# Up-projection of both MLPs by one level of Strassen's scheme, in four rounds

## The chip, the core and the metric

The kernel runs on one core of a Trainium2 chip. Its time is the device time of one execution in microseconds (us), taken on the chip; lower is better. TensorE (PE, with its weight loads as PEld) multiplies, VectorE (DVE) and ScalarE (ACT) work elementwise, GpSimd (POOL) does little here, and SyncE (SP) issues the transfers.

## The reference

Two layers over 16 meta tokens and 512 real ones, model width 1024, hidden width 4096, all in float32. Each layer is a mixer (stick-breaking attention in layer 0, a gated linear recurrence in layer 1) and then an MLP; a last norm closes it. What is changed is the MLP:

```python
def sq_relu_mlp(x, w_up, w_down):
    hdn = jax.nn.relu(x @ w_up)
    return (hdn * hdn) @ w_down
for i in range(DEPTH):
    ...
    hn = rms_norm(h, norm_mlp[i])
    h = h + sq_relu_mlp(hn, mlp_w_up[i], mlp_w_down[i])
h = rms_norm(h, norm_final)
return h[:, N_META:]
```

## The kernel before, in words

Activations lie transposed: the 1024 channels are 8 chunks of 128 partitions, the tokens are columns. Layer 0 works on all 528 columns, as two blocks of 264 (`ALL`, since one PSUM bank holds 512 floats); the second MLP and the output need the 512 real columns alone (`REAL`), one block of 512.

A float32 product is made of three fp32r products. `split` (L56 to L61) makes a rounded high part on ACT (L58) and the remainder on DVE (L61); `gemm` (L100) issues high by high, high by low and low by high for each 128x128 weight tile, all of them at L98. `load_unit` (L88) loads 512 KB of weights, 128 by 1024, into one of three `raw` buffers and splits it into `whi` and `wlo` (two buffers each).

At the end of the attention layer the output projection writes the residual stream: `hs<-z` or `hs<-g` at L545, per chunk of 128 channels and block of 264 columns. Per chunk `xs_write` scales by the gain and splits (ACT L128, DVE L129), and `Norm.add` squares on ACT and accumulates on DVE (L152). These eight pairs of `x` tiles are the input of the first MLP. The norm's factor `rstd` (L154 to L160: a product with ones, a square root on ACT, a reciprocal on DVE) is multiplied in after the first product.

`mlp` (L583) has two halves of 16 hidden chunks. In the up phase of a half each of 16 units gives one hidden chunk: 48 matmuls of 264 columns in layer 0 or 24 of 512 in layer 1, then `t` = max(g, 0)·rstd on DVE (L605), two squares on ACT (L608, L609) and `hl` on DVE (L610). In the down phase each of the 8 output chunks takes 16 hidden chunks, two units, and is added to `hs` (L637). In the very last chunk of layer 1 the two column halves are worked one after the other, and `last` (L804) makes the final norm, the multiplications (L829, L831) and the output transfers (L834) of each half.

Instructions are written in program order, and a scheduler interleaves them by priorities; what it arrived at is fixed when the kernel is built. Each engine then takes its queue strictly in that order. Weight loads and splits are raised in priority (`HP`).

Of the kernel before, what the change touches and what calls it, by code (L numbers as in the profile page):

```python
# [40 lines left out]
def tile_hybrid_trunk(ctx: ExitStack, tc: tile.TileContext, h0, vec, wqk, wv, wo, wob,  # L42
# [120 lines left out]
    xs_mlp0 = []  # L163
    hs = [None, None]

    def h_chunk(c):
        return hs[c // 4][:, c % 4, :]

    def attention_layer():
# [394 lines left out]
        x4 = [vqp.tile([P, 4, T], F32R, tag=t, name="x4") for t in ("v2", "v2", "q", "q")]  # L564
        xs_mlp0.append([x4[c // 4][:, c % 4, :] for c in range(KC)])
        xs_mlp0.append([x4[2 + c // 4][:, c % 4, :] for c in range(KC)])
        xs["h"], xs["l"] = xs_mlp0

        def final(m):
            xs_write(m, h_chunk(m), V_MLP0)  # L570
            nrm.add(m, h_chunk(m))
# [10 lines left out]
    def mlp(l, cols, nrm, done, xh, xl, gtile, last=None):

        c0a = cols[0][0]
        nb = len(cols)
        cw = cols[0][1]
        with ExitStack() as c2:
            hp = c2.enter_context(tc.tile_pool(name="hid", bufs=1))
            r3 = None
            hh = [hp.tile([P, T], F32R, name=f"hh{f}") for f in range(16)]  # L590
            hl = [hp.tile([P, T], F32R, name=f"hl{f}") for f in range(16)]
            for half in range(2):
                for f in range(16):
                    hi, lo = load_unit(wup[l, 16 * half + f])
# [1 line left out]
                    gemm([g[:, i, 0:w] for i, (_, w) in enumerate(cols)], cols,
                         [(hi[:, k * P:(k + 1) * P], lo[:, k * P:(k + 1) * P], xh[k], xl[k]) for k in range(KC)])
                    if r3 is None:
                        gs = gtile()
                        rstd = nrm.finish([gs[:, i, 0:w] for i, (_, w) in enumerate(cols)], cols)  # L600
                        r3 = rstd[:, c0a:T].rearrange("p (b w) -> p b w", b=nb)
                    t = hp.tile([P, T], F32, tag="t", name="t", bufs=2)
                    t3 = t[:, c0a:T].rearrange("p (b w) -> p b w", b=nb)
                    for i in range(nb):
                        dve.scalar_tensor_tensor(out=t3[:, i, :], in0=g[:, i, 0:cw], scalar=0.0, in1=r3[:, i, :],  # L605
                                                 op0=ALU.max, op1=ALU.mult)
                    r = hp.tile([P, T], F32, tag="r", name="r", bufs=2)
                    act.activation(out=hh[f][:, c0a:T], in_=t[:, c0a:T], func=AF.Square)  # L608
                    act.activation(out=r[:, c0a:T], in_=t[:, c0a:T], func=AF.Square)  # L609
                    dve.tensor_tensor(out=hl[f][:, c0a:T], in0=r[:, c0a:T], in1=f32(hh[f][:, c0a:T]),  # L610
                                      op=ALU.subtract)
                for m in range(KC):
                    us = [load_unit(wdn[l, half, m, j]) for j in range(2)]
                    g = gtile()
                    ks = [(us[k // 8][0][:, (k % 8) * P:(k % 8 + 1) * P], us[k // 8][1][:, (k % 8) * P:(k % 8 + 1) * P],
                           hh[k], hl[k]) for k in range(16)]
                    if last and half == 1 and m == KC - 1:
                        gs = [g[:, 0, 0:S // 2], gtile()[:, 0, 0:S // 2]]
                        cs = [NM, NM + S // 2]
                        gemm([gs[0]], [(cs[0], S // 2)], ks)  # L620
                        fin = [last(i, gtile()) for i in range(2)]
                        n = (0, 3, 8, 16)
                        for i in range(2):
                            next(fin[i])
                        for i in range(2):
                            hc = h_chunk(m)[:, cs[i]:cs[i] + S // 2]
                            b = ()
                            with tc.high_priority(HP * i):
                                dve.tensor_tensor(out=hc, in0=gs[i], in1=hc, op=ALU.add)
                                for j in range(3):  # L630
                                    if i == 0:
                                        gemm([gs[1]], [(cs[1], S // 2)], ks[n[j]:n[j + 1]], j == 0, j == 2, b)
                                    b = next(fin[i], ())
                        continue
                    gemm([g[:, i, 0:w] for i, (_, w) in enumerate(cols)], cols, ks)
                    h3 = h_chunk(m)[:, c0a:T].rearrange("p (b w) -> p b w", b=nb)
                    dve.tensor_tensor(out=h3, in0=g[:, 0:nb, 0:cw], in1=h3, op=ALU.add)  # L637
                    if half == 1:
                        done(m, h_chunk(m))
# [257 lines left out]
```

## Time and profile before

| | us |
|---|---|
| median of three runs | 1231.8 (1231.26 to 1233.49) |
| the profiled execution | 1233.84 |
| its span, first to last instruction | 1231.9 |
| PE busy in the span | 1205.1 |
| DVE busy | 672.6 |
| ACT busy | 558.4 |

The granted clock of TensorE has a mean of 0.993 over the span. The first MLP runs from 329.64 us to about 704.8, the second from 862.9 to 1221.7; the attention layer lies before, the recurrent mixer and its output projection between them. Busy times are of the records' own durations; since matmuls and DVE instructions overlap with their successors, the distance from one start to the next is what a queue of them takes.

### The profile page before, as it was taken

The page shows a single profiled execution, that of the slowest core. Times are in us where ns is not written, and L with a number is a line of the kernel's source. Part 1 is how long each engine was busy: PE and PEld are TensorE (multiplying, and loading weights), DVE is VectorE, ACT ScalarE, POOL GpSimd, SP SyncE. Part 2 cuts the span into 40 slices and gives each one's busy share as a digit, 9 for nine tenths or more (in the row PEclk, how much of TensorE's full clock was granted, in tenths as well). Part 3 has the DMA queues.
Part 4 walks back from the last instruction along what each step waited for, and adds up shares of the span by engine and source line. Part 5 has one row for each costly group of instructions (what it writes and reads, how often), then busy time and mean ns, then how long its engine had stood idle before and what let it go on. Part 6 is the DMA issues. An engine that isn't in the chain of part 4 may idle for free.

```text
span 1231.9 us, 19086 instructions
## 1 busy us (share of the span) xinstructions
PE 1205.1 (98%) x7932; PEld 1110.6 (90%) x7932; DVE 672.6 (55%) x1121; ACT 558.4 (45%) x927; POOL 15.5 (1%) x33
## 2 busy tenths in 40 slices
PE   7999999999999999999999999999999999999997
PEld 7999999998999999999999998878888888888886
DVE  7887878796754432344433487585544223444333
ACT  6777777786533311133323348663434121433321
POOL 3000000000000000000000000000000000000000
PEclk9999999999999999999999999999999999999998
DMA  6221213042223222322323231223232233232322
GB/s 219 85 82 57 82 35 89 17 122 69 87 89 101 87 86 87 103 86 87 99 74 103 86 120 63 75 69 119 87 101 88 86 103 103 86 103 86 103 86 69
DMA packets 33334, 110.14 MB, mean 89 GB/s; under 512 B 3936, under 2 KB 5984, under 8 KB 33248
## 3 DMA queue, kind: packets, MB, share of 16 engines
q1 hardware_dynamic: 32816, 108.53, 27.7%
q8 instruction: 62, 1.02, 0.3%
q10 hardware_dynamic: 432, 0.39, 0.1%
q14 instruction: 24, 0.20, 0.1%
HBM read 102.49 MB, written 2.10 MB: 85 GB/s over the span
## 4 chain that ended last, share of the span: by engine, by line
PE 90%; DVE 5%; ACT 3%; issue 2%; DMA 1%; SPq 0%; DVEq 0%; ACTq 0%
PE g L98 79%; PE z L98 9%; PE o L98 2%; DVE wlo L61 1%; ACT whi L58 1%; DVE th L715 1%; ACT r L79 0%; DVE i L714 0%; DMA hs<-in_h_dram 0%; DVE xl L129 0%; ACT th L79 0%; DVE y L749 0%; DMA q<-q 0%; ACT L79 0%; DVE rstd L159 0%
## 5 line engine op out<-in xcount | busy, mean ns | idle before, releaser
L58 ACT ACTIVATE whi<-raw 128x1024 fp32r<-128x1024 f32 (+1 forms) x178 | 186.7, 1050 | 550.3 <-PE g L98 288.0
L61 DVE TENSOR_TENSOR wlo<-raw,whi 128x1024 fp32r<-128x1024 f32 (+1 forms) x178 | 215.6, 1212 | 257.2 <-PE g L98 131.8
L98 PE MATMUL g<-xh,whi 128*128 128x264 f32 (+1 forms) x720 | 230.5, 335 | 0.5 <-DVE v L354 0.4
L98 PE MATMUL g<-xl,whi 128*128 128x264 f32 (+1 forms) x720 | 230.4, 334 | 0.0
L98 PE MATMUL g<-hh,whi 128*128 128x264 f32 (+2 forms) x784 | 229.3, 318 | 0.0
L98 PE MATMUL g<-hl,whi 128*128 128x264 f32 (+2 forms) x784 | 229.2, 318 | 0.0
L98 PEld LDWEIGHTS g<-hl,whi 128*128 128x128 f32 x784 | 147.5, 188 | 11.2
L98 PE MATMUL g<-xh,wlo 128*128 128x264 f32 (+1 forms) x720 | 156.8, 335 | 0.8 <-DVE wlo L61 0.8
L98 PEld LDWEIGHTS g<-hh,whi 128*128 128x128 f32 x784 | 147.6, 188 | 10.8
L98 PEld LDWEIGHTS g<-xh,whi 128*128 128x128 f32 x720 | 135.9, 189 | 15.2 <-PE z L98 0.5
L98 PEld LDWEIGHTS g<-xl,whi 128*128 128x128 f32 x720 | 135.9, 189 | 14.0 <-issue 0.2
L605 DVE SCALAR_TENSOR_TENSOR t<-g,rstd 128x264 f32<-128x264 f32 (+1 forms) x96 | 46.7, 515 | 172.4 <-PE g L98 172.3
L98 PE MATMUL g<-x,whi 128*128 128x264 f32 x1024 | 137.5, 284 | 0.8 <-DVE hs L545 0.8
L98 PE MATMUL g<-hh,wlo 128*128 128x264 f32 (+2 forms) x784 | 136.7, 319 | 0.0
L98 PEld LDWEIGHTS g<-x,whi 128*128 128x128 f32 x1024 | 130.7, 188 | 1.1 <-ACT sq L151 1.0
L98 PEld LDWEIGHTS g<-xh,wlo 128*128 128x128 f32 x720 | 117.5, 188 | 15.0 <-DVE wlo L61 1.1
L98 PEld LDWEIGHTS g<-hh,wlo 128*128 128x128 f32 x784 | 115.5, 188 | 10.8
L98 PE MATMUL g<-x,wlo 128*128 128x264 f32 x512 | 78.4, 285 | 0.0
L98 PEld LDWEIGHTS g<-x,wlo 128*128 128x128 f32 x512 | 69.2, 188 | 0.1
L79 ACT ACTIVATE sp<-sp 128x288 f32<-128x288 f32 (+3 forms) x128 | 62.2, 510 | 1.3
L98 PE MATMUL g<-vhi,xl 128*128 128x256 f32 x160 | 46.1, 289 | 0.0
L98 PE MATMUL g<-vhi,xh 128*128 128x256 f32 x160 | 46.1, 288 | 0.0
(189 smaller groups left out, 1607.4 us busy)
## 6 DMA issues: line engine op xcount, KB each, us to landing
raw<-in_wup_dram SPq DMA_DIRECT2D x64, 512.0 KB, 3.3
raw<-in_wdn_dram SPq DMA_DIRECT2D x64, 512.0 KB, 3.3
raw<-in_win_dram SPq DMA_DIRECT2D x16, 512.0 KB, 3.4
raw<-in_wqk_dram SPq DMA_DIRECT2D x14, 512.0 KB, 3.5
q<-q SPq DMA_DIRECT2D x16, 264.0 KB, 4.5
raw<-in_wv_dram SPq DMA_DIRECT2D x8, 512.0 KB, 3.4
raw<-in_wo_dram SPq DMA_DIRECT2D x8, 512.0 KB, 3.4
raw<-in_wout_dram SPq DMA_DIRECT2D x8, 512.0 KB, 3.3
```

The source lines that it names most:

```text
L58: act.activation(out=hi, in_=src, func=AF.Copy)
L61: (lo_eng or dve).tensor_tensor(out=lo, in0=src, in1=f32(hi), op=ALU.subtract)
L79: ins = act.activation(out=out, in_=in_, func=func, **kw)
L98: return pe.matmul(out=o, lhsT=lhsT, rhs=rhs, start=start, stop=stop, skip_group_check=True)
L605: dve.scalar_tensor_tensor(out=t3[:, i, :], in0=g[:, i, 0:cw], scalar=0.0, in1=r3[:, i, :], op0=ALU.max, op1=ALU.mult)
L715: dve.tensor_tensor_scan(out=ths[n], data0=rs[n], data1=is_[n], initial=0.0, op0=ALU.mult, op1=ALU.add)
```

## The change

The up-projection `x @ w_up` is cut into 2 by 2 blocks: the 1024 input channels into an upper and a lower half of 4 chunks, two hidden chunks at a time (a pair), the token columns into two blocks of 264 (layer 0) or 256 (layer 1, `HALVES`). Instead of eight block products a pair takes seven, in the form with 15 additions that is due to Winograd. Each block product is 4 chunks by 3 fp32r products, 12 matmuls; a pair has 84.

- `Blocks` makes the inputs' operands: `B11`, `B21` (scaled columns), `N22` (a negated block) and the differences `T1` to `T4`, each split into high and low. It takes the place of `xs_write` at the end of the attention layer and of the mixer. Chunk k and chunk k+4 go together; `upper` does the first, `lower` the second.
- `up_weights` makes a pair's weight operands: of two loaded units the sums `S1`, `P2`, `P3`, `P4`, split like the others.
- `up_pair` issues the products into four accumulators a, b, d, c (two PSUM tiles), combines them through `u2` and `v` on DVE, applies `rstd`, and squares.
- The MLP has four rounds, each of 4 pairs (8 hidden chunks) and a down phase of 8 output chunks with 8 hidden chunks each. The down products keep their number; `hs` is added to 32 times a layer instead of 16.
- At the end of the last round output chunks 6 and 7 are worked by column halves: 6 and 7 of the first half, then 6 and 7 of the second.
- Buffers: `vqp` lives through the kernel and its tiles are shared by tags, the slots of `xh`/`xl` also hold `hh`/`hl` and mixer tiles, high and low parts of the attention's `s` and `w` share one tile. One attention mask is a slice of another, three POOL instructions less. The host lays `w_down` out by rounds.

The core of the diff; of the old `mlp` only the listing above is shown:

```diff
+    class Blocks:
...
+        def scaled(self, c, h_c, x):
+            (a, w), _ = self.cols
+            act.activation(out=x, in_=h_c[:, a:a + 2 * w].rearrange("p (b w) -> p b w", b=2), func=AF.Copy,
+                           scale=vecs[:, self.g0 + c:self.g0 + c + 1])
+        def upper(self, k, h_c):
+            w = self.cols[0][1]
+            x2 = pair(6, [P, 4, HT], F32, "x2")
+            self.x, self.y = x2[:, 0:2, 0:w], x2[:, 2:4, 0:w]
+            self.d = pair(7, [P, 4, HT], F32, "t4")[:, :, 0:w]
+            self.scaled(k, h_c, self.x)
+            dve.tensor_tensor(out=self.d[:, 0, :], in0=self.x[:, 1, :], in1=self.x[:, 0, :], op=ALU.subtract)
+            split(self.x[:, 0, :], *self.op["B11"][k])
+            split(self.d[:, 0, :], *self.op["T1"][k])
+        def lower(self, k, h_c):
+            x, y, d = self.x, self.y, self.d
+            self.scaled(4 + k, h_c, y)
+            dve.tensor_tensor(out=d[:, 1, :], in0=y[:, 1, :], in1=d[:, 0, :], op=ALU.subtract)
+            dve.tensor_tensor(out=d[:, 2, :], in0=x[:, 1, :], in1=y[:, 1, :], op=ALU.subtract)
+            dve.tensor_tensor(out=d[:, 3, :], in0=y[:, 0, :], in1=d[:, 1, :], op=ALU.subtract)
+            hi, lo = self.t[k]
+            split(d[:, 1:4, :], hi[:, 1:4, :], lo[:, 1:4, :])
+            split(y[:, 0, :], *self.op["B21"][k])
+            hi, lo = self.op["N22"][k]
+            act.activation(out=hi, in_=y[:, 1, :], func=AF.Copy, scale=-1.0)
+            dve.scalar_tensor_tensor(out=lo, in0=y[:, 1, :], scalar=-1.0, in1=f32(hi), op0=ALU.mult, op1=ALU.subtract)
...
+            if m in (0, 1, 2, 3):
+                blocks.upper(m, h_chunk(m))
+            if m in (0, 1, 2, 7):
+                blocks.lower(m % 4, h_chunk(m % 4 + 4))
+            nrm.add(m, h_chunk(m))
...
+            def up_weights(p):
+                with tc.high_priority(HP):
+                    a1, a2 = (wp.tile([P, 2 * H], F32, tag="raw", name="raw", bufs=3) for _ in range(2))
+                    for i, a in enumerate((a1, a2)):
+                        nc.sync.dma_start(out=a, in_=wup[l, 2 * p + i])
...
+                    split(a1, *hl_[0])
+                    dve.tensor_tensor(out=pq[:, H:], in0=a1[:, 0:H], in1=a2[:, 0:H], op=ALU.add)
+                    dve.tensor_tensor(out=a2[:, 0:H], in0=a2[:, 0:H], in1=a2[:, H:], op=ALU.add)
+                    split(a2, *hl_[1])
+                    dve.tensor_tensor(out=pq[:, 0:H], in0=a2[:, 0:H], in1=a1[:, 0:H], op=ALU.add)
+                    split(pq, *hl_[2])
+                    dve.tensor_tensor(out=p4, in0=pq[:, 0:H], in1=a1[:, H:], op=ALU.add)
+                    split(p4, *hl_[3])
...
+            def up_pair(p, hid):
+                W = up_weights(p)
+                g1, g2 = gtile(), gtile()
+                a, b, d, c = (g[:, i, 0:w] for g in (g1, g2) for i in range(2))
+                def prod(o, left, right, start):
+                    hi, lo = W[left]
+                    for k in range(4):
+                        x, xl_ = op[right][k]
+                        mm(o, hi[:, k * P:(k + 1) * P], x, start and k == 0, False)
+                        mm(o, hi[:, k * P:(k + 1) * P], xl_, False, False)
+                        mm(o, lo[:, k * P:(k + 1) * P], x, False, k == 3)
...
+                prod(a, "A11", "B11", True)
+                act.activation(out=n1, in_=a, func=AF.Copy)
+                yield
+                prod(d, "S1", "T1", True)
+                yield
+                prod(b, "P2", "T2", True)
+                dve.tensor_tensor(out=u2, in0=b, in1=n1, op=ALU.subtract)
+                prod(c, "P3", "T3", True)
+                v = t[:, 3, :]
+                dve.tensor_tensor(out=v, in0=c, in1=u2, op=ALU.add)
+                dve.tensor_tensor(out=v, in0=d, in1=v, op=ALU.add)
+                prod(a, "A12", "B21", False)
+                r3 = st["r3"]
+                dve.scalar_tensor_tensor(out=t[:, 0, :], in0=a, scalar=0.0, in1=r3[:, 0, :], op0=ALU.max, op1=ALU.mult)
+                prod(c, "A22", "T4", False)
+                prod(d, "P4", "N22", False)
+                for i, x in enumerate((d, c)):
+                    dve.tensor_tensor(out=t[:, 1 + i, :], in0=x, in1=u2, op=ALU.add)
+                dve.scalar_tensor_tensor(out=t[:, 1, :], in0=t[:, 1, :], scalar=0.0, in1=r3[:, 1, :],
+                                         op0=ALU.min, op1=ALU.mult)
+                dve.scalar_tensor_tensor(out=t[:, 2:4, :], in0=t[:, 2:4, :], scalar=0.0, in1=r3,
+                                         op0=ALU.max, op1=ALU.mult)
+                for i in range(2):
+                    h_, l_ = (x[:, c0a:T].rearrange("p (b w) -> p b w", b=2) for x in hid[i])
+                    x = t[:, 2 * i:2 * i + 2, :]
+                    act.activation(out=h_, in_=x, func=AF.Square)
+                    act.activation(out=x, in_=x, func=AF.Square)
+                    dve.tensor_tensor(out=l_, in0=x, in1=f32(h_), op=ALU.subtract)
+                yield
...
+            for q in range(4):
+                gens = [up_pair(4 * q + j, [(hh[2 * j + i], hl[2 * j + i]) for i in range(2)]) for j in range(4)]
+                if q == 0:
+                    next(gens[0])
+                    next(gens[0])
+                    next(gens[1])
+                    gs = gtile()
+                    rstd = nrm.finish([gs[:, i, 0:w] for i in range(2)], cols)
+                    st["r3"] = rstd[:, c0a:T].rearrange("p (b w) -> p b w", b=2)
+                for g in gens:
+                    for _ in g:
+                        pass
+                first = [(down_ks(q, m), gtile()) for m in range(2)]
+                for part in (slice(0, 6), slice(6, 8)):
+                    for m, (ks, g) in enumerate(first):
+                        gemm(down_outs(g), dcols, ks[part], part.start == 0, part.stop == 8)
+                        if part.stop == 8:
+                            down_end(q, m, g)
...
+    mlp(1, HALVES, REAL, nrm, blocks, done1, gtile, last)
```

Three places show how the order of the queues moves.

DVE where the attention layer ends and the first MLP begins, before: `hs` sums (L545), `x4` splits (L129), the norm's `acc` (L152), and a weight split (L61).

```order
L152 TENSOR_TENSOR acc_4071<-acc_4071,sq_4330 128x528
L545 TENSOR_TENSOR hs_3868<-g_4341,hs_3868 128x264
L129 SCALAR_TENSOR_TENSOR x4_4074<-hs_3868,vecs_70,x4_4072 128x528
L545 TENSOR_TENSOR hs_4078<-z_4388,xr_4354 128x264
L152 TENSOR_TENSOR acc_4071<-acc_4071,sq_4351 128x528
L61 TENSOR_TENSOR wlo_4535<-raw_4532,whi_4534 128x1024
L129 SCALAR_TENSOR_TENSOR x4_4075<-hs_4078,vecs_70,x4_4073 128x528
L152 TENSOR_TENSOR acc_4071<-acc_4071,sq_4416 128x528
```

The same place now, the last rows up to the split of `T2` to `T4` of the fourth chunk pair (`xt_3941`, 792 wide): `t4` are the differences, `pq`, `p4` and `o1l`, `o2l` the second pair's weight sums and splits.

```order
L66 TENSOR_TENSOR xb_3945<-x2_4263,xb_3945 128x264
L225 SCALAR_TENSOR_TENSOR xn_3947<-x2_4263,xn_3947 128x264
L210 TENSOR_TENSOR t4_4264<-x2_4263 128x264
L218 TENSOR_TENSOR t4_4264<-x2_4263 128x264
L665 TENSOR_TENSOR pq_4434<-raw_4431,raw_4430 128x512
L217 TENSOR_TENSOR t4_4264<-x2_4263,t4_4264 128x264
L66 TENSOR_TENSOR o1l_4439<-raw_4431,o1_4438 128x1024
L66 TENSOR_TENSOR xt_3941<-t4_4264,xt_3941 128x264
L667 TENSOR_TENSOR p4_4435<-pq_4434,raw_4430 128x512
L219 TENSOR_TENSOR t4_4264<-x2_4263,t4_4264 128x264
L66 TENSOR_TENSOR o2l_4441<-pq_4434,o2_4440 128x1024
L66 TENSOR_TENSOR xt_3941<-t4_4264,xt_3941 128x792
```

Weight operands and input operands now alternate in one queue. From the first `hs<-z` of the output projection to the last row shown there are 78 instructions: 8 of 1024 columns, 4 of 792, 7 of 528, 9 of 512, and 50 of 264, two of these reciprocals.

PE at the start of the first MLP, before: any chunk's products of one unit follow one another.

```order
L98 MATMUL g_4538<-x4_4072,whi_4534 128x264
L98 MATMUL g_4538<-x4_4074,whi_4534 128x264
L98 MATMUL g_4538<-x4_4073,whi_4534 128x264
L98 MATMUL g_4538<-x4_4075,whi_4534 128x264
L98 MATMUL g_4538<-x4_4073,whi_4534 128x264
```

Now: the first two pairs interleaved (`g_4400`, `g_4401` hold a, b, d, c of the first, `g_4456`, `g_4457` of the second).

```order
L103 MATMUL g_4401<-xt_3940,o2l_4385 128x264
L103 MATMUL g_4457<-xt_3941,o1_4438 128x264
L103 MATMUL g_4457<-xt_3941,o1l_4439 128x264
L103 MATMUL g_4457<-xt_3938,o2_4440 128x264 x2
L103 MATMUL g_4400<-xt_3941,o2_4384 128x264
L103 MATMUL g_4401<-xt_3941,o2_4384 128x264
L103 MATMUL g_4456<-xt_3938,o2l_4441 128x264
L103 MATMUL g_4456<-xt_3939,o2_4440 128x264 x2
L103 MATMUL g_4456<-xt_3939,o2l_4441 128x264
```

The row that takes `o2l_4441`, the second pair's weight split that DVE makes second to last in the rows above, is the 75th matmul of the MLP; the 91st takes the low part of the 792-wide split.

DVE at the end of the kernel, before: the first column half's multiplications (`hg`) stand ahead of the second half's last sum (`hs_4078<-g_11865`).

```order
L629 TENSOR_TENSOR hs_4078<-g_11864,hs_4078 128x256
L819 RECIPROCAL rt_9669<-rt_9669 128x2
L823 TENSOR_SCALAR dg_9670<-identf_9665,rt_9669 128x128 x2
L831 TENSOR_TENSOR hg0_9657<-g_11914,hg0_9657 128x256
...
L829 SCALAR_TENSOR_TENSOR hg7_9664<-hs_4078,vecs_70,g_11914 128x256
L629 TENSOR_TENSOR hs_4078<-g_11865,hs_4078 128x256
L819 RECIPROCAL rt_9669<-rt_9669 128x2
L823 TENSOR_SCALAR dg_9670<-identf_9665,rt_9669 128x128 x2
L831 TENSOR_TENSOR hg0_9657<-g_11915,hg0_9657 128x256
```

Now both halves' factors come first, and the multiplications of both stand at the very end.

```order
L779 TENSOR_TENSOR hs_3950<-g_12849,hs_3950 128x256
L987 RECIPROCAL rt_9742<-rt_9742 128x2
L991 TENSOR_SCALAR dg_12679<-identf_9739,rt_9742 128x128 x2
L167 TENSOR_TENSOR acc_9738<-acc_9738,sq_12934 128x256
L779 TENSOR_TENSOR hs_3950<-g_12850,hs_3950 128x256
L987 RECIPROCAL rt_9742<-rt_9742 128x2
L991 TENSOR_SCALAR dg_12679<-identf_9739,rt_9742 128x128 x2
L999 TENSOR_TENSOR hg_12675<-g_12851,hg_12675 128x256 x4
L999 TENSOR_TENSOR hg_12676<-g_12851,hg_12676 128x256
L997 SCALAR_TENSOR_TENSOR hg_12676<-hs_3950,vecs_73,g_12851 128x256
L999 TENSOR_TENSOR hg_12675<-g_12852,hg_12675 128x256 x4
```

Twelve multiplications and their transfers thus stand behind the second half's last sum, where six stood.

## Rows read from the trace of the kernel before

**Rows 1.** The page: busy time per engine; the chain of work that ended last, by engine.

```profile
PE 1205.1 (98%) x7932; PEld 1110.6 (90%) x7932; DVE 672.6 (55%) x1121; ACT 558.4 (45%) x927; POOL 15.5 (1%) x33
...
PE 90%; DVE 5%; ACT 3%; issue 2%; DMA 1%; SPq 0%; DVEq 0%; ACTq 0%
```

**Rows 2.** Windows: us, then busy us (count) of PE, PEld, DVE, ACT, POOL; clock; DMA.

```profile
310.85:329.64 18.79, 17.97 (x146) 17.64 (x145) 17.31 (x32) 12.51 (x18) 0.00 (x0) 1.00 0.35 114
329.64:424.09 94.45, 94.45 (x772) 94.32 (x773) 45.62 (x66) 35.55 (x51) 0.00 (x0) 1.00 0.28 90
424.09:517.50 93.41, 93.41 (x768) 93.41 (x767) 25.81 (x26) 18.05 (x18) 0.00 (x0) 1.00 0.27 85
```

**Rows 3.** Timeline of PE, both MLPs: start us, duration, instruction, count, idle before.

```profile
329.64 1.45 PE L98 MATMUL g<-x,whi 128*128 128x264 f32 x10 [0.82 <-DVE hs L545]
...
342.33 0.53 PE L98 MATMUL g<-x,whi 128*128 128x264 f32 x3
...
348.17 0.41 PE L98 MATMUL g<-x,whi 128*128 128x264 f32 x2
...
874.83 0.39 PE L98 MATMUL g<-xh,whi 128*128 128x512 f32 x1
...
880.35 0.39 PE L98 MATMUL g<-xh,whi 128*128 128x512 f32 x1
...
1208.34 0.28 PE L98 MATMUL g<-hh,whi 128*128 128x256 f32 x1
...
1214.02 0.61 PE L98 MATMUL g<-ones,acc 128*128 128x1 f32 x5
```

**Rows 4.** Timeline of DVE at the end of the attention layer.

```profile
310.85 1.48 DVE L545 TENSOR_TENSOR hs<-z,xr 128x264 f32<-128x264 f32 x4 [2.22 <-PE z L98]
312.25 0.42 DVE L545 TENSOR_TENSOR hs<-g,hs 128x264 f32<-128x264 f32 x1
312.59 1.21 DVE L61 TENSOR_TENSOR wlo<-raw,whi 128x1024 fp32r<-128x1024 f32 x1
313.72 0.42 DVE L545 TENSOR_TENSOR hs<-g,hs 128x264 f32<-128x264 f32 x1
...
316.90 0.69 DVE L152 TENSOR_TENSOR acc<-acc,sq 128x528 f32<-128x528 f32 x1
317.52 0.76 DVE L129 SCALAR_TENSOR_TENSOR x<-hs,vecs,x 128x528 fp32r<-128x528 f32 x1
```

**Rows 5.** Lines by form, DVE: total us, mean ns of one, idle before.

```profile
L159 DVE RECIPROCAL rstd<-rstd 128x264 f32<-128x264 f32 x6 | 10.8, 1792 | 1.4 <-ACT rstd L79 1.4
```

**Rows 6.** Timeline of DVE at the start of the second MLP.

```profile
863.12 0.69 DVE L762 TENSOR_TENSOR hs<-g,hs 128x512 f32<-128x512 f32 x1 [2.23 <-PE g L98]
...
871.50 3.35 DVE L159 RECIPROCAL rstd<-rstd 128x512 f32<-128x512 f32 x1 [0.78 <-ACT rstd L79]
874.89 1.29 DVE L605 SCALAR_TENSOR_TENSOR t<-g,rstd 128x512 f32<-128x512 f32 x2
876.10 1.21 DVE L61 TENSOR_TENSOR wlo<-raw,whi 128x1024 fp32r<-128x1024 f32 x1
```

**Rows 7.** Timeline of ACT at the same place.

```profile
869.49 1.28 ACT L79 ACT_TABLE_LOAD   x1
870.78 0.69 ACT L79 ACTIVATE rstd<-g,eps 128x512 f32<-128x512 f32 x1
```

**Rows 8.** Timeline of DVE at the end of the kernel.

```profile
1219.27 1.75 DVE L831 TENSOR_TENSOR hg<-g,hg 128x256 f32<-128x256 f32 x5 [1.69 <-ACT rb L825]
...
1225.99 1.75 DVE L831 TENSOR_TENSOR hg<-g,hg 128x256 f32<-128x256 f32 x5 [1.75 <-ACT rb L825]
```

**Rows 9.** Windows in the attention layer around a wait of PE, columns as in rows 2.

```profile
288.00:292.00 4.00, 1.95 (x8) 1.14 (x7) 3.21 (x6) 3.97 (x10) 0.00 (x0) 1.00 0.69 195
292.00:296.00 4.00, 3.37 (x13) 3.15 (x13) 3.24 (x7) 2.04 (x4) 0.00 (x0) 0.57 0.18 72
```

**Rows 10.** The page, transfers: issue, count, size, us from issue to landing.

```profile
raw<-in_wup_dram SPq DMA_DIRECT2D x64, 512.0 KB, 3.3
```

More of the change, by code (lines that the diff above doesn't have):

```diff
@@ L439, in do_o @@
                 table(out=x[:, 0:w], in_=zt[:, 0:w], func=AF.Exp, tset=LNEXP)
-                ws = two(x, w, "wh", "wl", 2, act if t else dve, dve)
+                wt = pair(7, [P, 2, S], F32R, "w") if turn("w", 2) else ap_.tile([P, 2, S], F32R, tag="w", name="w")
+                ws = two(x, w, wt, act if t else dve, dve)
                 if t == 3:
@@ L563, in attention_layer @@
         nrm = Norm()
[L564 to L571, printed above, removed]
+        blocks = Blocks(V_MLP0, ALL)
         for m in (4, 5, 0, 1, 6, 2, 3, 7):
@@ L587, in mlp @@
+        return nrm, blocks
+    def mlp(l, cols, dcols, nrm, blocks, done, gtile, last=None):
+        c0a, w = cols[0]
+        nb, cw = len(dcols), dcols[0][1]
+        H = KC * P // 2
         with ExitStack() as c2:
             hp = c2.enter_context(tc.tile_pool(name="hid", bufs=1))
[L589 to L594, printed above, removed]
-                    g = gtile()
[L596 to L639, printed above, removed]
@@ new lines, in mixer, with gtile, done0 @@
+        return nrm2, blocks
+    with ExitStack() as ctx_a:
+        nrm, blocks = attention_layer()
+    mps = ctx.enter_context(tc.tile_pool(name="mps", bufs=4, space=PSUM))
+    def gtile():
+        return mps.tile([P, 2, S], F32, tag="g", name="g")
+    nrm1 = Norm()
+    xm = []
+    def done0(c, h_c):
+        if not xm:
+            x4 = quads([P, 4, T], F32R, "xm")
+            xm.extend([x4[2 * i + k // 4][:, k % 4, :] for k in range(KC)] for i in range(2))
+            xs["h"], xs["l"] = xm
+        xs_write(c, h_c, V_MIX1)
+        nrm1.add(c, h_c)
@@ new lines, in tile_hybrid_trunk, with gain, done1 @@
+    mlp(0, ALL, ALL, nrm, blocks, done0, gtile)
+    nrm, blocks = mixer(nrm1, *xm, gtile)
+    nrm3 = Norm(NM)
+    identf = const.tile([P, P], F32, name="identf")
+    pool.memset(identf, 1.0)
+    pool.affine_select(out=identf, in_=identf, pattern=[[-1, P]], base=0, channel_multiplier=1,
+                       compare_op=ALU.is_equal, fill=0.0)
+    rt = const.tile([P, 4], F32, name="rt")
+    hg, ft = [], {}
+    def gain(c):
+        return vecs[:, V_FIN + c:V_FIN + c + 1]
+    def done1(c, h_c, cols=slice(NM, T)):
+        if not hg:
+            t4 = [vqp.tile([P, 4, S], F32, tag="v2", name="hg") for _ in range(2)]
+            hg.extend(t4[k // 4][:, k % 4, :] for k in range(KC))
+            ft["sq7"], ft["rb"] = (pair(0, [P, 2, S], F32, "sq7")[:, i, :] for i in range(2))
+            ft["dg"] = pair(1, [P, 4, P], F32, "dg")
+        nrm3.add(c, h_c, cols)
+        act.activation(out=hg[c][:, cols.start - NM:cols.stop - NM], in_=h_c[:, cols], func=AF.Copy, scale=gain(c))
```

239 lines of the change are left out of this document (144 added, 95 removed).

## The prediction, made before the changed kernel was run

> **What bounds the kernel now.** I read the busy times first. PE works 1205.1 us of a span of 1231.9, and the chain of work that ended last lies on PE for 90%, on DVE for 5% [rows 1]. So the kernel is bound by the number of matmuls, and time goes where PE has fewer of them or has to wait. Then the windows, for what else each stage holds: in the first MLP PE has no gap (93.41 of 93.41 us for 768 matmuls) while DVE works 25.81 us in the up phase's second part and 45.62 of 94.45 in the first window [rows 2]. There DVE and ACT have much room. Just ahead of it they have none: from 310.85 to 329.64 DVE works 17.31 of 18.79 us [rows 2], and PE's only wait there, 0.82 us at 329.64, is for DVE's `hs` [rows 3]. So the interior can pay for additions, and the edge between the attention layer and the MLP can't. The timelines give the prices: a matmul of 264 columns is (348.17 - 342.33)/48 = 0.1217 us, of 512 columns (880.35 - 874.83)/24 = 0.230, of 256 columns (1214.02 - 1208.34)/48 = 0.1183 [rows 3].
>
> On DVE what counts in a full queue is the distance between starts. 264 columns: 312.25 to 312.59, and the next start after 313.72 is 0.34 on; I take 0.345. 1024 columns: 312.59 to 313.72, 1.13. 528: 316.90 to 317.52, 0.62 [rows 4]. 512: two from 874.89 to 876.10, 0.605, taken as 0.60 [rows 6]. For 792 and 256 no row stands; between 264 and 528 a column costs 0.275/264 = 1.04 ns, which gives 0.895 and 0.335. A reciprocal of 264 takes 1.79 [rows 5].
>
> **Products removed and added.** Layer 0's up phase had 32 units of 48 matmuls, 1536 of 264 columns; now 16 pairs of 84, 1344. That removes 192 x 0.1217 = 23.4 us. Layer 1 had 32 x 24 = 768 of 512 columns, now 1344 of 256: 768 x 0.230 - 1344 x 0.1183 = 176.6 - 159.0 = 17.6 us. An eighth of the columns goes, and part of that is lost since two of 256 cost more than one of 512. The down products stay as many and as wide. Sum: **-41.0 us** of PE. This term is sure; all else is what is given back.
>
> **Operands at the start of the first MLP.** Before, the input needed per chunk one split of 528 columns (L129), finished with the norm's sums. Now each pair of chunks asks DVE for four differences, four 264-wide splits and one of 792, and the first two pairs' weight operands (three 1024-wide splits, one 512-wide, four 512-wide sums each) stand in the same queue. From the first `hs<-z`, which starts at 310.85 [rows 4], to the split of `T2` to `T4` of the fourth pair of chunks there are 78 instructions by the order: 48 of 264 x 0.345 = 16.6; 8 of 1024 x 1.13 = 9.0; 7 of 528 x 0.62 = 4.3; 4 of 792 x 0.895 = 3.6; 9 of 512 x 0.60 = 5.4; 2 reciprocals x 1.79 = 3.6. Together 42.5 us, done at 353.4; the second to last, `o2l` of the second pair, at 352.5. PE comes to the MLP at 329.64 [rows 3] and its 75th matmul there takes that `o2l`: 74 x 0.1217 = 9.0 us, at 338.6. It is 13.9 us early. DVE waits on its own: in the 18.79 us before the MLP it stood 1.5 us [rows 2], and here the stretch is more than twice as long and the reciprocals stand behind a table load (1.28 us in rows 7) and a square root; I take 3. **+17 us**, bounds 11 (the scheduler's interleaving leaves some sums ahead of their wait) and 24 (each engine in turn waits for the other). Behind PE's wait the whole rest of round 0 is queued, but it takes PE longer than DVE: the pairs' outputs and the other two pairs' weights are 4 x 4.28 + 2 x 6.39 + 2.3 = 32 us on DVE (terms below) against some 245 matmuls, 30 us, and the first down chunks, 8.8 us. So no second stall there.
>
> The Trainium skill (VectorE: DVE Perf Modes, on the drain that can't be avoided) has it that a DVE instruction doesn't start before the one ahead has left the pipe. By the durations alone the trace would seem to agree, 0.42 us for 264 columns and 1.21 for 1024, but the starts disagree: they lie 0.34 and 1.13 apart [rows 4]. A dependent pair does wait: the reciprocal at 871.50 lasts 3.35 and what reads it starts at 874.89 [rows 6]. By the rule the 78 instructions would take 78 x 0.085 = 6.6 us more.
>
> **Operands and outputs in the rounds.** Per pair on DVE: weights 3 x 1.13 + 5 x 0.60 = 6.39, outputs 7 x 0.345 + 3 x 0.62 = 4.28, together 10.67 us, against 84 x 0.1217 = 10.22 of PE. In the up phase alone DVE would be late. But the first pair's weights are made in the down phase before it, and the first two down chunks use their first 6 hidden chunks (72 matmuls, 8.8 us) before they need the last pair's. So DVE has 3 x 6.39 + 4 x 4.28 + 2 x 1.13 = 38.5 us to do in 40.9 + 8.8 = 49.7. In the down phase it has little (8 x 1.13 + 8 x 0.62 = 14 us in 46.7). ACT does per pair three conversions of 1024, one of 512, one copy and four squares of 528, less than DVE. I take about 1 us per round for waits at seams, **+5** for both layers' eight rounds after the starts (bounds 0 and 30, the latter under the rivals). Loads: two units a pair, landing in 3.3 us [rows 10]; the same 64 as before, on SP's queue with nothing else there.
>
> **Start of the second MLP.** From the last `hs` sum at 863.12 [rows 6] DVE has 18 instructions to the second pair's `o2l`, that sum among them: 3 of 1024 x 1.13, 6 of 512 x 0.60, 7 of 256 x 0.335 and 2 reciprocals of 256 at half the 3.35 of one of 512 [rows 6]: 12.7 us, done at 875.8. PE has 74 products of 256 columns and two of the norm's, 9.0 us from 863.0, to 872.0. Late 3.8; the table load and square root (1.28 and 0.69 [rows 7]) stand ahead of the reciprocals, and before the change DVE stood 0.78 there [rows 6]; I add 3: **+7**, bounds 3 and 14. Its stretch is shorter since the mixer's output chunks are further apart (5.6 us each).
>
> **Attention.** Its tiles for `s` and `w` now hold both parts, so the scheduler frees them together and the order shifts late in the stage. Nothing is removed or added but three POOL instructions. **+2**, bounds -3 and +8: that stage already has waits of PE, such as 2.05 us in 288 to 292 [rows 9], which can shrink or grow.
>
> **Tail.** The first half's six multiplications on DVE, 1.75 us for the five and 0.4 for the sixth [rows 8], stood in the 48 matmuls of the second half and now stand behind its last sum; a good part fits into the wait of 1.75 us ahead of the second half's [rows 8]. The transfers of the first half are issued behind that too. **+2.5**, bounds 0 and 5.
>
> **Clock.** After the wait at 288 to 292 the granted clock of the next 4 us is 0.57 [rows 9], the lower level of 1.2 GHz for most of it: 0.43 x 4 = 1.7 us lost. The first start has such a wait for certain, the second perhaps: **+2**, bounds 0 and 5.
>
> **Sum.** -41.0 + 17 + 5 + 7 + 2 + 2.5 + 2 = -5.5. Against the profiled execution, 1233.84 (its span of 1231.9 and 1.9 around it, which stay), that is 1228.3; that execution stands 2.0 above the median of 1231.8, so 1226.3 on the median's scale. I say 1227.
>
> **Rivals.** (a) The starts are hidden: the scheduler's queue lets PE do more products with the operands that are ready, and the 24 us of starts with the 2 of the clock shrink to nothing. -31.5, 1200. For it: PE has 1300 other matmuls to do in the layer. Against it: the order is fixed, and the 75th matmul names its operand. 6%.
>
> (b) The drain of whole DVE durations holds wherever queue neighbours share a tile, as differences and splits do: 6.6 us more at the first start, 1 at the second. In the rounds a pair's weights are then 3 x 1.21 + 5 x 0.69 = 7.1 and its outputs 7 x 0.42 + 3 x 0.69 = 5.0 [rows 4, 6], the up work 3 x 7.1 + 4 x 5.0 + 2 x 1.21 = 43.7 us, still under 49.7. Sum +2.1, 1234 on the median's scale. [...] 17%, since the rows show it for dependent neighbours alone.
>
> (c) Slower: DVE sets the pace of every up phase. `pq` and `p4` have one buffer each and `raw` three, so a pair's second load waits until the last sum of the pair before has read `raw`, and takes 3.3 us [rows 10] that no DVE work fills if the queue is in strict order. Three such waits, 9.9, on the 43.7 by durations make 53.6 us in place of 49.7, +3.9 for each of the six later rounds, and one wait of 3.3 in the two first: +30 in place of +5, so about 1251. It decides from 49.7 us of DVE up work and waits per round. For it: DVE at 10.67 a pair is slower than PE's 10.22. Against it: loads are issued early, and DVE can be ahead by a pair since the operand tiles have two buffers. 22%.
>
> (d) The change does less than it says: by the counts the products are 84 a pair. Excluded.
>
> **Chances.** My forecast 55%: its own range is 1215 to 1239 from the two starts' bounds. (a) 6, (b) 17, (c) 22. The range 1208 to 1249 takes in all but most of (a) and the upper half of (c). What the measurement can tell from no change is 0.2%, 2.5 us, so faster is under 1229.3. From the forecast 46 of 55 and all of (a) and 2 of (b) are faster: 54; the same are 5 of the forecast and 14 of (b), 19; slower 4, 1 and (c) 22: 27.
>
> **What would show it.** Right: in the windows of the first MLP PE loses 15 to 20 us within 15 us of its start, waiting for DVE splits of `o2l` or `xt`, and then has no gap of more than 1 us until the mixer; the up phase of a later round takes 41 us; the second start shows 5 to 10 us. Wrong for the rate: pairs that are not 10.2 and 9.9 us long on PE. Rival (c) shows as a wait for DVE in every round, longest ahead of a pair's `S1` or `P2` products; (a) as a first MLP without gap; (b) as DVE starts that lie whole durations apart. A longer attention stage or tail by over 8 us would also make it wrong.

## The result, and the profile after

The changed kernel takes 1222.74 us (four runs, 1221.41 to 1224.14), the kernel before 1231.8 (1231.26 to 1233.49). A fourth run of the kernel before, at 1680.92 us, was in a slow state and is left out. The ratio of the others is 0.9924, 95% interval 0.9904 to 0.9943: faster by 7 to 12 us. The forecast was 1227, with a range of 1208 to 1249. The profiled executions differ by 12.2 us in span, 1231.9 to 1219.7, and so by 3 more than the medians: the one before lies 2.0 above its median, the one after 1.3 below. First the page after, its busy times and the chain of work that ended last, which answer to [rows 1]:

```profile
PE 1171.8 (96%) x8318; PEld 1105.6 (91%) x8318; DVE 892.1 (73%) x1564; ACT 642.7 (53%) x1066; POOL 12.5 (1%) x30
...
PE 83%; DVE 9%; ACT 5%; issue 2%; DMA 1%; SPq 0%; DVEq 0%; ACTq 0%
```

DVE works 219.5 us more and takes 9% of the chain instead of 5%: it now stands on the path at some places. Which, the timeline of PE shows (start us, duration, instruction, count, idle before):

```profile
330.34 0.48 PE L103 MATMUL g<-xb,whi 128*128 128x264 f32 x2 [0.62 <-DVE hs L604]
...
333.60 0.56 PE L103 MATMUL g<-xb,whi 128*128 128x264 f32 x1 [2.29 <-ACT xb L63]
335.40 0.59 PE L103 MATMUL g<-xb,whi 128*128 128x264 f32 x1 [1.25 <-DVE xb L66]
...
342.88 0.71 PE L103 MATMUL g<-acc,ones 128*128 128x264 f32 x2 [1.89 <-ACT rstd L84]
345.56 0.81 PE L103 MATMUL g<-xb,whi 128*128 128x264 f32 x2 [1.97 <-ACT xb L63]
348.15 0.59 PE L103 MATMUL g<-xb,whi 128*128 128x264 f32 x1 [1.78 <-DVE xb L66]
...
349.84 1.25 PE L103 MATMUL g<-xt,o 128*128 128x264 f32 x4 [0.44 <-ACT o L63]
...
359.52 0.48 PE L103 MATMUL g<-xb,whi 128*128 128x264 f32 x2
...
435.70 0.41 PE L103 MATMUL g<-xb,whi 128*128 128x264 f32 x2
...
702.90 3.32 PE L103 MATMUL g<-xm,whi 128*128 128x264 f32 x26
...
859.19 0.40 PE L103 MATMUL g<-xb,whi 128*128 128x256 f32 x2
...
867.91 0.70 PE L103 MATMUL g<-acc,ones 128*128 128x256 f32 x2 [1.51 <-ACT rstd L84]
...
874.06 0.38 PE L103 MATMUL g<-xt,o2l 128*128 128x256 f32 x1 [2.05 <-DVE o2l L66]
```

The first MLP starts at 330.34, and at 359.52 PE has done the 98 matmuls that stand ahead of that row in its order (100 records, since each of the norm's two products leaves two). At 0.1217 us they take 11.9, and they took 29.2: 17.3 us are lost. The waits after the first add up to 9.6 us. Most of the other 7.7 are matmuls at half the clock, 1.2 GHz: some 45 of them start 0.22 us apart instead of 0.12, which is 4.5 us. The rest lies around the waits. Windows of the same kernel show the clock (columns as in [rows 2], clock third from the end):

```profile
330.30:349.80 19.50, 9.89 (x37) 7.83 (x37) 19.09 (x31) 13.62 (x24) 0.00 (x0) 0.67 0.17 55
...
350.00:352.00 2.00, 2.00 (x10) 2.00 (x11) 2.00 (x4) 1.71 (x4) 0.00 (x0) 0.50 0.00 0
...
356.00:358.00 2.00, 2.00 (x19) 2.00 (x18) 1.93 (x3) 0.00 (x0) 0.00 (x0) 1.00 0.24 96
...
768.00:772.00 4.00, 4.00 (x23) 3.48 (x24) 4.00 (x6) 1.98 (x3) 0.00 (x0) 1.00 0.10 42
772.00:776.00 4.00, 4.00 (x24) 3.51 (x23) 3.96 (x8) 1.30 (x2) 0.00 (x0) 1.00 0.40 131
```

DVE works 19.09 of the first 19.50 us, so I take it that DVE sets the pace there and that PE's waits, whoever they are put down to, are shares of its queue; e1 and v1 below test that. Here is that queue's beginning and end, and two later places:

```profile
311.95 0.77 DVE L604 TENSOR_TENSOR hs<-z,xr 128x264 f32<-128x264 f32 x2
...
353.35 1.21 DVE L66 TENSOR_TENSOR o2l<-pq,o 128x1024 fp32r<-128x1024 f32 x1
354.49 0.97 DVE L66 TENSOR_TENSOR xt<-t,xt 128x792 fp32r<-128x792 f32 x1
...
424.08 0.69 DVE L662 TENSOR_TENSOR pq<-raw 128x512 f32<-128x512 f32 x1 [3.58 <-DMA raw<-in_wup_dram]
...
1204.86 0.48 DVE L991 TENSOR_SCALAR dg<-identf,rt 128x128 f32<-128x128 f32 x2
...
1207.72 0.42 DVE L779 TENSOR_TENSOR hs<-g,hs 128x256 f32<-128x256 f32 x1 [2.04 <-PE g L103]
...
1209.79 0.95 DVE L991 TENSOR_SCALAR dg<-identf,rt 128x128 f32<-128x128 f32 x2
```

From the first `hs` to the end of the 792-wide split, where the next start would be (0.895 after 354.49), it is 43.4 us; the hand sum was 42.5.

Stage by stage the span's 12.2 us are: attention 0.7 later; the first MLP, from its first matmul to the mixer's first, 372.6 instead of 375.2 (704.84 - 329.64); mixer and output projection 156.3 instead of 158.1; the second MLP up to its last `hs` sum 348.5 instead of 358.8; the tail behind that 12.0 instead of 10.2. So layer 0 gained 1.9 us, and the second MLP with the tail 8.5. The mixer's 1.8 us are a drop of the clock that isn't in this execution: the two windows from 768 above have 1.00, those of the kernel before

```profile
768.00:772.00 4.00, 2.55 (x12) 2.35 (x13) 4.00 (x6) 2.14 (x4) 0.00 (x0) 0.81 0.39 135
772.00:776.00 4.00, 4.00 (x15) 3.14 (x15) 4.00 (x7) 1.21 (x2) 0.00 (x0) 0.77 0.34 119
```

The drop comes and goes without the change. In e2 below, whose mixer is that of the kernel before, both windows have 1.00. In f3, whose mixer is that of the changed kernel, the drop is there, and mixer and output projection take 157.9 us (703.55 to 861.47):

```profile
768.00:772.00 4.00, 3.45 (x14) 3.17 (x15) 4.00 (x6) 2.57 (x5) 0.00 (x0) 0.63 0.29 113
772.00:776.00 4.00, 4.00 (x18) 3.26 (x17) 3.96 (x7) 0.03 (x1) 0.00 (x0) 0.95 0.37 131
```

### The profile page after: what moved, and what is told of

Same layout as the page of the kernel before. It is cut to its first block, busy times and chain, and to the rows that moved or that the text cites. A ratio compares the mean times of both kernels' runs of the same rounds, so it can differ in the third digit from the quotient of the medians.

```text
span 1219.7 us, 20415 instructions
## 1 busy us (share of the span) xinstructions
PE 1171.8 (96%) x8318; PEld 1105.6 (91%) x8318; DVE 892.1 (73%) x1564; ACT 642.7 (53%) x1066; POOL 12.5 (1%) x30
## 4 chain that ended last, share of the span: by engine, by line
PE 83%; DVE 9%; ACT 5%; issue 2%; DMA 1%; SPq 0%; DVEq 0%; ACTq 0%
PE g L103 73%; PE z L103 8%; PE o L103 2%; ACT whi L63 2%; DVE wlo L66 1%; DMA raw<-in_wqk_dram 1%; DVE rstd L174 1%; DVE th L878 1%; ACT r L84 0%; DVE acc L167 0%; DVE i L877 0%; ACT L84 0%; DVE xl L144 0%; ACT th L84 0%; DVE th L912 0%
## 5 line engine op out<-in xcount | busy, mean ns | idle before, releaser
L103 PE MATMUL g<-xt,o 128*128 128x264 f32 (+1 forms) x1024 | 191.3, 286 | 0.9 <-ACT n L696 0.5
L103 PEld LDWEIGHTS g<-xt,o 128*128 128x128 f32 x1024 | 160.3, 191 | 2.0 <-ACT o L63 0.7
L103 PEld LDWEIGHTS g<-hh,wlo 128*128 128x128 f32 x784 | 120.3, 188 | 10.1
L103 PE MATMUL g<-xb,whi 128*128 128x264 f32 (+1 forms) x512 | 98.8, 289 | 8.8 <-ACT xb L63 4.3
L103 PEld LDWEIGHTS g<-xb,whi 128*128 128x128 f32 x512 | 80.6, 191 | 11.8 <-ACT xb L63 4.9
L103 PE MATMUL g<-xt,o1l 128*128 128x264 f32 (+1 forms) x256 | 73.2, 286 | 0.1
L103 PE MATMUL g<-xb,wlo 128*128 128x264 f32 (+1 forms) x256 | 73.2, 286 | 0.0
L103 PE MATMUL g<-xt,o2l 128*128 128x264 f32 (+1 forms) x256 | 71.0, 284 | 2.1 <-DVE o2l L66 2.1
L103 PE MATMUL g<-xh,whi 128*128 128x264 f32 x272 | 72.1, 287 | 0.8 <-DVE v L412 0.4
L103 PE MATMUL g<-xl,whi 128*128 128x264 f32 x272 | 72.0, 286 | 0.0
L103 PE MATMUL g<-xm,whi 128*128 128x264 f32 (+1 forms) x384 | 67.3, 322 | 0.1
```

Of the source, the lines that this page charges most:

```text
L103: return pe.matmul(out=o, lhsT=lhsT, rhs=rhs, start=start, stop=stop, skip_group_check=True)
```

## The experiments

"After" is the changed kernel, 1222.74 us. Ratios are against the kernel before, run on the same chip; their 95% interval stands behind them.

**Is it DVE's queue that the first start waits for? (e1)** Layer 0's input operands lose their low parts: the kernel leaves out the DVE splits and multiplies the high parts twice.

```diff
+            self.low = g0 != V_MLP0
+            if not self.low:
+                self.op = {n: [[x[0], x[0]] for x in v] for n, v in self.op.items()}
+        def split(self, src, hi, lo):
+            if self.low:
+                split(src, hi, lo)
+            else:
+                act.activation(out=hi, in_=src, func=AF.Copy)
...
-            split(d[:, 1:4, :], hi[:, 1:4, :], lo[:, 1:4, :])
+            self.split(d[:, 1:4, :], hi[:, 1:4, :], lo[:, 1:4, :])
```

> The changed kernel without the low parts of layer 0's input operands: the high part stands in for each low one, so PE has the same products and DVE 20 splits less (4 times 0.345 x 4 + 0.895 = 9.1 us) at the first start. Theory (DVE's queue sets the 17.0 us lost at the first start): about 9 us less, 1213.5, start loss 8. Rival (the table load, the square root and PE's own order set it): under 2 us less, 1221 to 1223.

Measured 1212.68, ratio 0.9842 (0.9828 to 0.9857): 10.1 us less than after. PE has the same matmuls; the first MLP takes 361.7 us (331.63 to 693.30) instead of 372.6. The rival falls: table load (1.28 us at 343.20) and square root were still there. In the window of the start, 1.3 us shorter than the one above, PE now does 98 matmuls where it did 37:

```profile
331.60:349.80 18.20, 15.17 (x98) 13.92 (x99) 17.98 (x25) 12.90 (x21) 0.00 (x0) 0.91 0.38 116
```

**Do the rounds alone gain? (e2)** The kernel before with plain products, in four rounds.

```diff
-            for half in range(2):
-                for f in range(16):
+            for q in range(4):
+                for f in range(8):
...
+                first = [(down_ks(q, m), gtile()) for m in range(2)]
+                for part in (slice(0, 6), slice(6, 8)):
```

> The kernel before with plain products, in four rounds of 8 hidden chunks and down phases of 8 (the first two output chunks begun with 6 hidden chunks): no Strassen. Theory (the rounds alone are free, 16 more sums a layer of 0.62 us are hidden): 1232, within 2 us of before. Rival (part of the 10 us comes from the rounds): 1226 to 1229.

1234.28, ratio 1.0016 (1.0006 to 1.0025): 2 us slower. One wait of PE for `sq` in the tail, where the last chunk has half as many products, went from 1.0 to 2.4 us. The rounds alone give nothing.

**Which layer? (e3)** Layer 0 plain, in rounds; layer 1 as after.

```diff
+                if l == 0:
+                    gens = []
+                    for f in range(8):
+                        plain(8 * q + f, hh[f], hl[f])
```

> Seven products in layer 1 alone, layer 0 plain in four rounds. Theory (layer 0 removes 23.4 us and gives back 17.0 at its start and 3.8 in its rounds): 2 to 3 us slower than the changed kernel, 1225. Rival (the gain is spread evenly over the layers): 1227 to 1228.

1225.64, ratio 0.9954 (0.9937 to 0.9971): 2.9 more than after, as the theory has it. The interval alone, 1224 to 1228, doesn't shut out the rival; the stages do. The first MLP takes 375.6 us (332.77 to 708.41), 3.0 more than after, and the second 347.7 instead of 348.5. An eighth fewer products in layer 0 are worth 3 us there. The first MLP also starts 2.4 us later than after, for which no run was made.

**Can POOL take work off DVE? (e4, e5, p1)** e4 gives it the norms' sums, e5 the differences too; p1 adds work that nobody needs.

```diff
-                dve.tensor_tensor(out=self.acc[:, c], in0=self.acc[:, c], in1=sq[:, c], op=ALU.add)
+                self.eng.tensor_tensor(out=self.acc[:, c], in0=self.acc[:, c], in1=sq[:, c], op=ALU.add)
...
-        nrm = Norm()
+        nrm = Norm(eng=pool)
...
-            dve.tensor_tensor(out=d[:, 1, :], in0=y[:, 1, :], in1=d[:, 0, :], op=ALU.subtract)
+            pool.tensor_tensor(out=d[:, 1, :], in0=y[:, 1, :], in1=d[:, 0, :], op=ALU.subtract)
...
+            pool.tensor_tensor(out=t, in0=h_chunk(m)[:, 0:S], in1=h_chunk(m)[:, 0:S], op=ALU.mult)
```

The first two pairs of lines are in e4 and e5 (and the same for the norm of layer 1), the third, with the other three differences, in e5 alone, the last line in p1.

> The changed kernel with the norms' sums of squares ahead of both MLPs on POOL in place of DVE (7 of 0.62 us and 7 of 0.60 less on DVE). Theory (DVE's queue sets both starts): 4.3 us less at the first start and 2 to 4 at the second, 1215 to 1217. Rival (the norm's chain is what is waited for, and POOL takes about 1.4 us for each sum): no gain or slower, 1222 to 1226.

> The changed kernel with the norms' sums of squares and the operands' differences T1 to T4 on POOL, in both layers (16 of 0.345 us more off DVE at each start). Theory (DVE's queue): 9 us less at the first start and 4 at the second, about 1210. Rival (chains through POOL at 0.7 to 1.4 us a step take DVE's place): 1214 to 1222.

e4 took 1227.23 (0.9955, 0.9938 to 0.9972), e5 1230.57 (0.9985, 0.9975 to 0.9994): both slower than after, e4 by 4.5 us where 6 to 8 less were expected, e5 by 8 where 13 less were. The rivals had the sign, but not all of the mechanism: e4's first MLP starts 4.2 us later, at 334.55, after a wait of 3.25 us for DVE's `hs`, not for the norm. Timeline of POOL and of DVE in e4:

```profile
321.04 1.49 POOL L168 TENSOR_TENSOR acc<-acc,sq 128x528 f32<-128x528 f32 x1 [1.36 <-ACT sq L167]
```

```profile
320.93 0.42 DVE L218 TENSOR_TENSOR t<-x,t 128x264 f32<-128x264 f32 x1
321.27 1.56 DVE L226 SCALAR_TENSOR_TENSOR xn<-x,xn 128x264 fp32r<-128x264 f32 x1
322.75 0.42 DVE L66 TENSOR_TENSOR xb<-x,xb 128x264 fp32r<-128x264 f32 x1
```

`xn`, 264 columns, lasts 1.56 us instead of 0.42 and ends 0.3 after POOL's sum. A sum of 0.62 us that DVE was spared stopped it here for 1.1. DVE's order in e4 differs from the one in after, and to part this from the order, p1:

> The changed kernel with eight multiplications of 512 columns on POOL at the end of the attention layer, each of a chunk of hs with itself, whose results nothing reads. DVE's work up to the first MLP's operands is the same, 42.5 us by the order. Theory (while POOL reads SBUF, a DVE instruction with two SBUF inputs stands still, as the stretched rows of e4 and e5 suggest): up to 1.1 us for each that falls into DVE's busy stretch, 4 to 9 us slower than the changed kernel, 1227 to 1232. Rival (e4 and e5 were slower since the scheduler ordered DVE otherwise): 1221 to 1224.

1228.32, ratio 0.9971 (0.9961 to 0.9981): 5.6 us slower than after by work with no reader. DVE's order changed here too, but only behind the first 40 instructions from the first `hs<-z` on. Those 40 stand as in after, and they take 22.6 us (313.48 to 336.08) instead of 18.5 (311.95 to 330.45). POOL and DVE there:

```profile
315.16 5.00 POOL L636 TENSOR_TENSOR x<-hs 128x512 f32<-128x512 f32 x3 [298.99 <-DVE hs L604]
```

```profile
315.27 0.42 DVE L604 TENSOR_TENSOR hs<-g,hs 128x264 f32<-128x264 f32 x1
315.61 1.68 DVE L66 TENSOR_TENSOR wlo<-raw,whi 128x1024 fp32r<-128x1024 f32 x1
317.21 0.42 DVE L604 TENSOR_TENSOR hs<-g,hs 128x264 f32<-128x264 f32 x1
317.55 1.71 DVE L66 TENSOR_TENSOR wlo<-raw,whi 128x1024 fp32r<-128x1024 f32 x1
```

`hs`, with one operand in PSUM, keeps its 0.42; the splits, with both in SBUF, go from 1.21 to 1.7. POOL is held up as well: its three multiplications took 5.00 us here, and a later one by itself 1.04 (326.11). The Trainium skill (SBUF — State Buffer, on SBUF's two separate sides) says the same: a DVE instruction with two SBUF inputs and a GpSimd one that reads SBUF exclude each other through a shared port pair.

**How much room do the rounds have? (f1, f2, f3)** From the second round on each pair gets useless 1024-wide subtractions on DVE: two (shown), six, one.

```diff
                     split(p4, *hl_[3])
+                    if p >= 4:
+                        for _ in range(2):
+                            x = hp.tile([P, 2 * H], F32R, tag="x", name="x")
+                            dve.tensor_tensor(out=x, in0=pq, in1=f32(hl_[2][0]), op=ALU.subtract)
```

> The changed kernel with two more 1024-wide subtractions on DVE for each pair from the second round on, whose result nothing reads: 2.26 us a pair. Theory (a round's up work on DVE, 38.5 us, is hidden up to 49.7): 38.5 + 3 x 2.26 = 45.3, hidden, at most 3 us more, 1223 to 1226. Rival (DVE already sets the pace of the rounds): 6 rounds x 6.8 = 41 us more, 1260 and above.

> The same with six, 6.78 us a pair. Theory: 38.5 + 3 x 6.78 = 58.8 us, 9.1 over 49.7 in each of 6 rounds: 55 us more, 1278. Rival (operands are made further ahead than counted, so that a round's whole 87.6 us cover 56.7 + 27.1): at most 5 us more, 1228.

f1 took 1248.67 (1.0130, 1.0113 to 1.0147), 26 us more than after, f2 1341.32 (1.0886, 1.0870 to 1.0903), 119 more. That fits neither the theory (3 and 55) nor the rivals. The one long wait of PE in f1's second round:

```profile
471.55 0.51 PE L103 MATMUL g<-xt,o 128*128 128x264 f32 x2 [3.04 <-ACT o L63]
```

It stands inside the fourth pair, before its products with `S1`, and not at the round's end. Each of the six later rounds has it: 3.04 us in layer 0, 1.98 and 0.69 in layer 1, 17.1 in all. In the kernel after, a round's first weight operand is made at 424.08, when its load has landed (the row above: 3.58 us idle for `raw`), 11.6 us before PE begins the round at 435.70. So the fourth pair is due after 11.6 + 3 x 10.22 = 42.3 us, for four pairs of weights and some 2.5 of outputs, 36.3. By this estimate 6.0 are left. f1 takes 9.0, 3.0 too many, and f2 27.1, 21.1 too many in each of six rounds, 127 where 119 were measured.

The estimate is rough, and that 3.0 meets the 3.04 measured is in part luck: it counts neither the 3.19 us that DVE stands idle at 443.20 for the third pair's load nor the `hs` sums and splits of the down phase, and the high part that PE waits for stands on ACT behind the squares. In f1 the 17.1 us of waits are two thirds of the 26. The mean clock fell from 0.988 to 0.983 over 1249 us, which is 6 more, and 3 stay open. In f2 PE waits at more places, 74 us in all for `o`, `t` and `u`, and the mean clock is 0.958. f3 put the new sum to the test:

> The changed kernel with one more 1024-wide subtraction on DVE a pair from the second round on (1.13 us). New theory, from the traces of the changed kernel and of f1: the deadline is the fourth pair's operands. DVE begins a round's operands 11.6 us ahead of PE, so it has 11.6 + 3 x 10.22 = 42.3 us for 4 x 6.39 of weights and about 2.5 x 4.28 of outputs, 36.3; 6.0 us are free, 1.5 a pair. 4 x 1.13 = 4.5 fits: at most 3 us more than the changed kernel, 1223 to 1226. Rival (no free time, each 2.26 a pair costs 26 as in f1): half of it, 1236.

1225.09, ratio 0.9943 (0.9926 to 0.9959): 2.3 more than after. The mixer's drop of the clock, shown above for its profiled execution, is 1.6 there. The new theory's forecast came, and its rival falls: one more subtraction a pair, 1.13 us, fits, and two, 2.26, don't. The terms of its sum are not tested one by one.

**A version without the first start (v1).** Layer 0's first round takes plain products, and DVE makes `T1` to `T4` and `N22` beside them.

```diff
+            def plain_round():
+                right = [[hp.tile([P, 4, HT], F32R, tag=t + x, name="b2", bufs=2) for x in ("", "l")] for t in ("o1", "o2")]
+                for c in range(KC):
+                    hi, lo = right[c // 4]
+                    blocks.direct(c, h_chunk(c), cols[1][0], hi[:, c % 4, :], lo[:, c % 4, :])
...
+                    if f < 6:
+                        blocks.rest(f - 2)
...
+                if l == 0 and q == 0:
+                    gens = []
+                    plain_round()
```

> The changed kernel with plain products in the first round of layer 0 alone: B12 and B22 are split at the start of the MLP, and the differences T1 to T4 and N22 are made in that round, where DVE has room. Theory (the first start loses 17.0 us to DVE's queue of operands): 17.0 less, 48 matmuls of 264 or 5.8 us more, about 1 for seams: 1212 to 1214, PE without a wait of over 1 us at the start. Rival (the differences come late for the second round, 38 us of DVE in 46.7 of PE): 1217 to 1222.

1212.87, ratio 0.9843 (0.9828 to 0.9858): 19 us under the kernel before, 9.9 under after, with 48 matmuls more. The first MLP takes 362.1 us (332.00 to 694.05). Of the 9.9, 1.3 are not layer 0's: the second MLP takes 347.2 us instead of 348.5, with a wait for `o2l` of 0.51 at its start in place of 2.05. PE's one wait at the start of the first, where none over 1 us was expected, is

```profile
332.00 1.95 PE L103 MATMUL g<-xb,whi 128*128 128x264 f32 x14 [1.65 <-ACT sq L166]
```

## Why the prediction was right, step by step

- **Products**, -41.0: right. The matmuls come at the rates of the kernel before: a later round of layer 0 takes 89.1 us (489.48 to 578.55), 1.5 more than its 720 matmuls at 0.1217, one of layer 1 84.6, 0.7 more than 336 at 0.1183 and 192 at 0.230.
- **First start**, +17 and most of +2 for the clock: 17.3 in all. The cause was right (e1, v1), and the price nearly so, but not the place. The step had PE wait at the 75th matmul, for `o2l`. It waited earlier, six times, for operands of the last two chunk pairs, for the norm's square root and for the second pair's `S1`, and then ran at half the clock up to 354. So it came to the 75th at 356.60, when `o2l` was there (354.49 by the next start). Taken by the step's own terms, `o2l` came 15.1 us after PE could have used it (330.34 + 9.0), not 16.9: of the 3 us that DVE was to stand on its own, the stretch shows 0.9 (43.4 for 42.5). What the clock added lies behind the last wait: the matmuls from 349.84 to 354 came at 0.22 us instead of 0.12, some 2 us. The slow matmuls before it cost nothing by this account, since the operands weren't ready; no run tests that by itself.
- **Rounds**, +5: after the first start layer 0 took 343.4 us for 2784 matmuls of 0.1217, 4.6 more than these; the first MLP before stood 1.2 over its own (375.2 for 3074), so 3.4 are new. Layer 1 lost about 3 (0.7 in each of four rounds). The size is near, but the step's cover, 38.5 us of DVE work in 49.7, was wrong: it set the deadline at the end of a round, and by it f1's 2.26 us a pair were hidden. PE waits at the fourth pair already, and the room lies between 1.13 us a pair (f3) and 2.26 (f1), not at 3.7 (11.2 over three pairs). That the work stayed hidden was closer than the text had it. Rival (c), with 22%, was that near, and DVE does stand idle for loads in layer 0's second round, 3.58 us at 424.08 and 3.19 at 443.20.
- **Second start**, +7: PE waits 4.3 us there, 2.05 of it for `o2l` as forecast and 1.51 for the square root. Oversized by 2.7; no drop of the clock followed.
- **Attention**, +2: 0.7. **Tail**, +2.5: 1.8.
- **Mixer**, taken as unchanged: 1.8 less, a drop of the clock in the profiled execution of the kernel before. Nothing in the change is meant for it, and by e2 and f3 the drop isn't the change's.
- **Rival (b)**, whole DVE durations: falls. The stretch took 43.4 us, where the rule gave 49, and starts of 264 columns still lie 0.34 apart, also where neighbours share a tile:

```profile
320.69 0.42 DVE L66 TENSOR_TENSOR xt<-t,xt 128x264 fp32r<-128x264 f32 x1
321.03 0.42 DVE L219 TENSOR_TENSOR t<-x,t 128x264 f32<-128x264 f32 x1
```

- **Rival (a)**: falls by the waits shown.

The terms as they came, -41.0 + 17.3 + 3.4 + 7.3 (layer 1: 358.8 - 17.6 would be 341.2, and it took 348.5) + 0.7 + 1.8 - 1.8, make -12.3; the spans differ by 12.2. The forecast's sum was -5.5. What was given back came out smaller nearly everywhere: the first start with the clock by 1.7, the second start by 2.7, attention by 1.3, the tail by 0.7; the rounds alone cost 1.4 more. So the saving was about twice the one forecast, on the medians 9.1 against 4.8, and it was the wide range that took it in.

Of the signs named beforehand, the loss of 15 to 20 us came, but over 29 us and not within 15, and the waits named are mostly for `xb`, not for `o2l` or `xt`. There was no later gap over 1 us in the first MLP, as forecast. The second start showed 4.3 us, where 5 to 10 were named. The forecast's own range, 1215 to 1239, should by the two starts' bounds have read 1217 to 1241.

## What to carry to other kernels

What is saved on the engine that bounds the kernel is paid where another engine has to prepare for it: count that engine's queue from the place where its inputs first exist to the row that is due, and set each deadline where the operand is first used, not at the end of a loop. Where a stage starts with such a queue, leave the first round on the old path and prepare beside it; that doubled the gain here. And an idle engine is help only if it doesn't share a port with the one that is full.

## What was not expected of the hardware

Neither the forecast nor the expectations of e4 and e5 had it that POOL's elementwise work on SBUF stops DVE instructions that have two SBUF operands: 0.42 us became 1.56 in e4, and 1.21 became 1.68 in p1, whereas sums with an operand in PSUM kept 0.42. The two `dg` instructions in the tail of the kernel after, with one full operand in SBUF and one scalar a partition, are stretched too, from 0.48 us at 1204.86 to 0.95 at 1209.79; POOL multiplied in SBUF from 1209.91 on. That is one case and no run was made for it.
